# Unused bytes between the on-chip tiles of a one-core encoder layer

## The chip, the core and the metric

The kernel runs on one core of one Trainium2 chip. The time is the device time of one execution in microseconds (us). The kernel before takes 2625.61 us (median of 3 runs, 2624.94 to 2625.66).

On-chip memory has 128 partitions, and a tile lies at the same byte range of each of them. Below, "place" is the byte at which a tile starts in a partition, and "residue" is that place modulo 512. The place of a tile isn't written in the kernel: tiles of a pool follow one another in the order in which their tags first appear, pools follow one another in the order in which they are opened, and a pool that is closed gives its place to the next.

## The reference

It is one encoder layer on 256 tokens of width 2048, all in float32: a half-step feed-forward block (SwiGLU with 5632 hidden columns), a mixer, a second half-step feed-forward block, and a layer norm behind each.

```
h = LN1(alpha*h + 0.5*SwiGLU_1(h))
h = LN2(alpha*h + Mixer(h))
h = LN3(alpha*h + 0.5*SwiGLU_2(h))

def swiglu(x, w_in, w_out):
    gate, up = jnp.split(x @ w_in, 2, axis=-1)
    return (jax.nn.silu(gate) * up) @ w_out
```

The mixer projects h to 18944 columns, runs a bidirectional gated linear recurrence (16 heads) and a dilated-window attention (12 heads) on them, projects both results back with `w_branch_a` and `w_branch_b`, gates and adds them, and ends with an output projection. Nearly all the arithmetic is activations (256 tokens) times float32 weights, which are read once.

## The kernel before

**Three products for one.** Each float32 operand a is split into H, which is a rounded to the type float32r, and L = a - H, also float32r. A product of x and W is computed as xH·WH + xH·WL + xL·WH, three matmuls that add up in one PSUM bank. TensorE loads a stationary operand of 128x128 (LDWEIGHTS) and streams a moving operand past it (MATMUL), one pair of instructions for each matmul.

**The stream of weights.** `run` goes through a list of `Job`s, one for each block of 512 or 1024 output columns. A job's weights come in chunks of 128 x 2048 elements (1 MB). `load` (L148 to L170) starts the DMA of a chunk into one of 3 `raw` tiles on SP's queue, and splits it in two halves: `nc.scalar.copy` writes `wH`, `nc.vector.tensor_sub` writes `wL` (both L165, four buffers each). `load` is called a step ahead of the matmuls that use it.

**Four forms of matmul.** In most jobs (`mm`, L217) the stationary operand is 128x128 of the transposed activations and the moving one is 128x512 of the weights:

- the projections of x: `xH` and `xL` are stationary;
- the second half of each feed-forward block: `hH` and `hL`, two buffers each, which hold the transposed hidden activations of a block;
- the projections behind the mixer: `oBH` and `oBL` (attention), `xH` and `xL` once more (recurrence), and `zH` and `zL` (output projection).

The projections to the attention's columns take every second token (`parity`), so that the stationary operand has a stride of two elements. The projections that feed the recurrence (`dims`, L229) are the other way round: 128x128 of the weights is stationary, and 128x256 of `xH` or `xL` moves. The last chunks of the second feed-forward half and of the output projection put their split weights outside the pool `wsp`, into tiles named `early` that lie in the same pool as `hH` and `hL`, or as `zL`.

**What else runs.** Between the matmuls of a job, `pump` places pieces of other work: transposes (`transpose4`, L104), the recurrence (L582 to L694) and the attention. ScalarE and VectorE split activations (`split`, L109 and L110), empty PSUM and do the layer norms. Three layer norms lie between the phases.

**Where tiles lie.** The pools `const`, `wraw`, `wsp`, `big` and `small` are opened once, in that order, and `ffn1`, `oA`, `hgrn`, `m2`, `att`, `m3` and `ffn2` lie behind them in turn. The first tile of the program, `ident` (512 bytes), lies at byte 16512, and the tiles of `const` add up to 3264 bytes, so that `raw` starts at 19776. All tiles of `wraw`, `wsp` and `big` are multiples of 4096 bytes. `small` takes 1248 bytes. So:

| tile | place before | residue | place after | residue |
|---|---|---|---|---|
| raw (first) | 19776 | 320 | 19456 | 0 |
| wH, wL | 44352 on | 320 | 44032 on | 0 |
| acc | 77120 | 320 | 76800 | 0 |
| xH | 93504 | 320 | 93184 | 0 |
| xL | 109888 | 320 | 109632 | 64 |
| first pool behind `small` | 127520 | 32 | 127488 | 0 |
| hH, two buffers (first feed-forward block) | 143904, 152096 | 32, 32 | 144512, 152768 | 128, 192 |
| hL, two buffers | 160288, 168480 | 32, 32 | 161024, 169280 | 256, 320 |
| oBH, oBL, zH, zL | | 32 | | 0 |
| early beside h | | 32 | | 0 or 384 |
| early beside z | | 32 | | 0 |

The column "after" follows from the sizes of the tiles in the change below.

Of the kernel before, what the change touches and what calls it, by code (L numbers as in the profile page):

```python
# [10 lines left out]
F32 = mybir.dt.float32  # L11
F32R = mybir.dt.float32r
# [5 lines left out]
P = 128  # L18
SEQ = 256
NT = SEQ // P  # L20
D = 2048
KD = D // P
# [20 lines left out]
class Job:  # L43
    """One block of output columns: out[tok, C] = sum over nk tiles of x^T W.

    head/tail: this many of the first/last chunks run one token tile after the other.
    room: gives room for a chunk's split weights outside the pool for them, or None.
    mid: called after the first step; hook: before the last token tile meets the last chunk.
    dims: the block comes out transposed, out[col, tok], two heads to a bank.
    """  # L50

# [18 lines left out]
def kernel(ctx, tc, x, ffn1_in, ffn1_out, ln1_g, ln1_b, mix_in, lb_fwd, lb_bwd,  # L70
# [3 lines left out]
    x, out = x[0], out[0]  # L74
# [3 lines left out]
    const = ctx.enter_context(tc.tile_pool(name="const", bufs=1))  # L78
    wraw = ctx.enter_context(tc.tile_pool(name="wraw", bufs=3))
    wsp = ctx.enter_context(tc.tile_pool(name="wsp", bufs=4))  # L80
    big = ctx.enter_context(tc.tile_pool(name="big", bufs=1))
    small = ctx.enter_context(tc.tile_pool(name="small", bufs=2))
# [9 lines left out]
    acc = big.tile([P, NT, D], F32, name="acc")  # L92

    def new_x():
        return (big.tile([P, KD, SEQ], F32R, tag="xH", name="xH"),
                big.tile([P, KD, SEQ], F32R, tag="xL", name="xL"))

# [9 lines left out]
    def split(ps, H, L):  # L107
        """H + L = ps exactly, both in float32r."""
        nc.scalar.copy(out=H, in_=ps)  # L109
        nc.vector.tensor_sub(out=L, in0=ps, in1=H.bitcast(F32))  # L110

    def rsqrt(y, v, n):
        """y = v ** -0.5 for [P, n] (v is positive): a guess from the exponent and three Newton steps."""
        z = small.tile([P, n], F32, tag=f"rs{n}", name="rsz")
        nc.vector.tensor_scalar(y.bitcast(I32), v.bitcast(I32), 1, None, op0=OP.logical_shift_right)
        nc.vector.tensor_scalar(y.bitcast(I32), y.bitcast(I32), -1.0, MAGIC, op0=OP.mult, op1=OP.add)
        for i in range(3):
            if n == 1:
                nc.vector.scalar_tensor_tensor(z, y, v, y, op0=OP.mult, op1=OP.mult)
            else:  # L120
                nc.vector.tensor_mul(z, y, y)
                nc.vector.tensor_mul(z, z, v)
            # the factor -2 of each of the first two steps stays in y, and is taken out in the last
            if i < 2:
                nc.vector.scalar_tensor_tensor(y, z, -3.0 * 4.0 ** i, y, op0=OP.add, op1=OP.mult)
            else:
                nc.vector.tensor_scalar(z, z, -768.0, -1.0 / 8192.0, op0=OP.add, op1=OP.mult)
                return nc.vector.tensor_mul(y, y, z)
# [17 lines left out]

# [1 line left out]
    def load(job, r, parts=1):  # L148
# [25 lines left out]
    def fence(ins):  # L174
        """What is traced from here to the end of this step or, if that is sooner, of the next
        goes to the vector engine behind ins."""
        es = ExitStack()
        es.enter_context(tc.issue_after(ins.ins))
        fences.append([es, 2])
# [95 lines left out]
    def to_x(src, xo, t, c):  # L275
        """Columns c * 512... of token tile t, in src [P, 512], to the transposed H and L."""
        ps = transpose4([src[:, i * P:(i + 1) * P] for i in range(4)])
        ts = slice(t * P, (t + 1) * P)
        split(ps.rearrange("p (k s) -> p k s", k=4), xo[0][:, 4 * c:4 * c + 4, ts], xo[1][:, 4 * c:4 * c + 4, ts])

# [1 line left out]
    stats = {}  # L282
# [6 lines left out]
    class LayerNorm:  # L289
# [32 lines left out]
        def tile(self, t):  # L322
            """Token tile t of acc is complete."""
            if t == 1:
                for c, u in self.got.items():
                    self.apply(0, c, u)
            self.begin(t)
            if t == 0:
                if not self.lead:
                    self.apply(0, 0)  # L330
            elif self.dst is not None:
                self.rest([(1, c) for c in range(4)])
            elif self.lead:
                self.rest([(1, 0), (1, 1), (0, 2), (1, 2), (0, 3), (1, 3)])
            else:
                self.rest([(1, 0)] + [(tt, c) for c in range(1, 4) for tt in range(NT)])

        def first(self):
            """The last tile is nearly complete."""
            for c in range(2 if self.dst is None else 4):  # L340
                self.got[c] = self.scale(0, c)
# [10 lines left out]

# [1 line left out]
    def ffn(w_in, w_out, cur, pool, before, tpost, post, hook):  # L354
        blocks = [(0, 512)] + [(c, 1024) for c in range(512, DFF, 1024)]
        jobs, outs = [], []
        for bi, (c0, C) in enumerate(blocks):
            st = {}

# [11 lines left out]
            def hid(st=st, C=C):  # L371
                st["H"] = pool().tile([P, 8, SEQ], F32R, tag="hH", name="hH", bufs=2)
                st["L"] = pool().tile([P, 8, SEQ], F32R, tag="hL", name="hL", bufs=2)

                def gen():
                    for c in range(C // 512):
                        for t in range(NT):
                            to_x(st["s"][:, t, c * 512:(c + 1) * 512], (st["H"], st["L"]), t, c)
                            yield 1.2
                fast.append(gen())  # L380
# [9 lines left out]
            last = bi == len(blocks) - 1  # L390
# [15 lines left out]
        last = jobs[-1]  # L406
        last.tail, last.room, last.tpost, last.post, last.hook = 4, room, tpost, post, hook
        return jobs

    cur = {}  # L410
    stacks = []
# [9 lines left out]

# [1 line left out]
    cur["x"] = new_x()  # L423
    pl = {}
    pl["ffn"] = open_pool("ffn1")
    vecs = const.tile([P, P], F32, name="vecs")

# [53 lines left out]

# [1 line left out]
    ln = {}  # L483
# [19 lines left out]

# [1 line left out]
    hs = {}  # L505
# [42 lines left out]
    def hgrn_pair(g, pr, st):  # L548
# [15 lines left out]
        def flat(ap, t, b, f):  # L564
            """[P, h * t, u] or, for one t, [P, h, u] of half f of block b."""
            if t is None:
                return ap.rearrange("p (g b f u) -> p g b f u", b=2, f=2, u=HCHUNK)[:, :, b, f, :]
            return v6(ap)[:, :, t, b, f, :]
# [7 lines left out]
        K1, Q1, KC, QC = t512("k1"), t512("q1"), t512("kc"), t512("qc")  # L576
        # direction d: inc is the decay from the chunk's entry up to and with a token, exc the decay
        # from behind a token to the chunk's end; entry and end are those of the direction's time
        KS, QR, inc, K2, Q2 = {}, {}, {}, {}, {}
        for d in range(2):  # L580
# [22 lines left out]
            yield 1.7  # L603
            # near half: the one that the direction enters first
            nr, fr = (0, 1) if d == 0 else (1, 0)
# [6 lines left out]
        for d in range(2):  # L612
            # keys of block bk meet queries of block bq of the same tile, keys of tile bk queries of tile bq
            nr, fr = (0, 1) if d == 0 else (1, 0)
# [28 lines left out]

        # scores, keys on partitions
        def tok(ap, h, t):
# [32 lines left out]
        for h in range(2):  # L678
            hl = 2 * pr + h
            hd = 4 * g + hl  # L680
            v = st["v"]
            for t in range(NT):
                o = po[:, (2 * h + t) * P:(2 * h + t + 1) * P]
                nc.tensor.matmul(out=o, lhsT=ATd[h][:, t, :], rhs=v[:, t, hl * P:(hl + 1) * P],  # L684
                                 start=True, stop=False)
                # ATo[:, h, 0]: keys of tile 0, queries of tile 1; [:, h, 1] the other way
                nc.tensor.matmul(out=o, lhsT=ATo[:, h, 1 - t, :], rhs=v[:, 1 - t, hl * P:(hl + 1) * P],  # L687
                                 start=False, stop=True)
# [70 lines left out]

    # attention: columns of group g are q, k, v of 512; tile 0 has the even tokens and tile 1 the odd ones,  # L760
    # so that the second and third group attend only within a tile
    def parity(x, k, t):
# [75 lines left out]

    # branch gates
    def gate_evac(key, blk):  # L840
# [99 lines left out]

# [1 line left out]
    def ln3_before():  # L942
# [57 lines left out]
```

## Time and profile before

| | |
|---|---|
| time, median of 3 runs | 2625.61 us |
| profiled execution, first to last instruction (its span) | 2623.6 us |
| TensorE (PE) busy | 2600.1 us, 99%, 12889 matmuls |
| weight loads (PEld) busy | 2187.8 us, 83% |
| VectorE (DVE) busy | 1533.4 us, 58% |
| ScalarE (ACT) busy | 1155.7 us, 44% |
| read from HBM | 479.17 MB, 183 GB/s over the span |
| granted TensorE clock, mean | 0.999 |

The page of the profile gives the busy time of each engine and a chain of work that ended last. The profiled execution is known by its span; the median of the runs is 2.0 us above it. A group of instructions is named by the line of the kernel, the engine, and "out<-in" by tile names, followed by its count, its busy time and the mean duration of one. A matmul is pipelined: its recorded duration is longer than the distance from its start to the start of the next. That distance, called spacing below, is read from the chain of waits, where a row "start, us, what xN" that holds N matmuls back to back has the length N times the spacing.

### The profile page before, as it was taken

To read this page: it belongs to the slowest core of one execution; us is meant where nothing else is said; L and a number is where in the kernel's file an instruction comes from. 1 tells how busy PE (TensorE), PEld (TensorE's weight loads), DVE (VectorE), ACT (ScalarE), POOL (GpSimd) and SP (SyncE) were. 2 spreads that over 40 slices of the span, in tenths; PEclk is the share of its full clock that TensorE was granted. 3 is DMA by queue.
4 is the path that set the end of the run, shared out by engine and by line. 5 is a ranking of instruction groups with operands and counts; after the bars stand their busy time and mean duration, and the time that the engine had idled before them with its cause. 6 is when DMAs were issued, how large, how long until landed. Compare 5 with 4: busy or idle time off the path is not lost.

```text
span 2623.6 us, 31518 instructions
## 1 busy us (share of the span) xinstructions
PE 2600.1 (99%) x12889; PEld 2187.8 (83%) x12889; DVE 1533.4 (58%) x1865; ACT 1155.7 (44%) x1395; POOL 4.8 (0%) x28
## 2 busy tenths in 40 slices
PE   8999999999999999999999999999999999999998
PEld 7888888888889999998888888888788888888886
DVE  5455555454585877878544544556755455555557
ACT  5444343444444455554544544444444444444442
POOL 0000000000000000000000000000000000000000
PEclk9999999999999999999999999999999999999999
DMA  7555555555655544544555445656555555555563
GB/s 243 187 184 192 192 192 179 193 190 192 211 174 177 177 162 145 174 163 161 188 177 183 154 162 193 191 191 213 172 193 191 193 178 192 191 192 181 193 220 129
DMA packets 147281, 483.32 MB, mean 184 GB/s; under 512 B 7664, under 2 KB 7872, under 8 KB 146368
## 3 DMA queue, kind: packets, MB, share of 16 engines
q1 hardware_dynamic: 145680, 473.99, 54.4%
q10 hardware_dynamic: 1456, 7.32, 0.7%
q8 instruction: 101, 1.65, 0.2%
q14 instruction: 44, 0.36, 0.0%
HBM read 479.17 MB, written 2.10 MB: 183 GB/s over the span
## 4 chain that ended last, share of the span: by engine, by line
PE 97%; DVE 2%; DMA 0%; ACT 0%; issue 0%; SPq 0%; DVEq 0%; ACTq 0%
PE ps L217 82%; PE ps L229 10%; PE tp L104 2%; PE tp L653 1%; PE tp L657 1%; DVE wL L165 0%; DVE lnu L307 0%; PE tp L687 0%; DVE lnu L311 0%; DMA acc<-in_x 0%; PE tp L808 0%; PE tp L816 0%; DVE st L287 0%; PE tp L684 0%; PE tp L672 0%; ACT wH L165 0%
## 5 line engine op out<-in xcount | busy, mean ns | idle before, releaser
L165 DVE TENSOR_TENSOR wL<-raw,wH 128x1024 fp32r<-128x1024 f32 x884 | 1078.1, 1222 | 1007.8 <-ACT wH L165 1006.3
L165 ACT CAST wH<-raw 128x1024 fp32r<-128x1024 f32 x884 | 929.0, 1052 | 1291.5 <-PE ps L217 1157.0
L217 PE MATMUL ps<-wH,xH 128*128 128x512 f32 x2336 | 748.1, 391 | 1.7 <-ACT xH L109 1.7
L217 PE MATMUL ps<-wL,xH 128*128 128x512 f32 x2336 | 749.0, 391 | 0.0
L217 PE MATMUL ps<-wH,xL 128*128 128x512 f32 x2336 | 748.6, 391 | 0.3
L217 PEld LDWEIGHTS ps<-wH,xH 128*128 128x128 f32 x2336 | 440.0, 189 | 92.5 <-ACT xH L109 2.8
L217 PEld LDWEIGHTS ps<-wH,xL 128*128 128x128 f32 x2336 | 440.2, 189 | 92.1 <-DVE xL L110 1.8
L217 PEld LDWEIGHTS ps<-wL,xH 128*128 128x128 f32 x2336 | 439.6, 189 | 89.9
L217 PE MATMUL ps<-wL,hH 128*128 128x512 f32 x672 | 216.7, 399 | 0.0
L217 PE MATMUL ps<-wH,hH 128*128 128x512 f32 x672 | 212.0, 396 | 0.0
L217 PE MATMUL ps<-wH,hL 128*128 128x512 f32 x672 | 210.9, 395 | 0.0
L217 PEld LDWEIGHTS ps<-wH,hL 128*128 128x128 f32 x672 | 126.0, 188 | 29.8
L217 PEld LDWEIGHTS ps<-wH,hH 128*128 128x128 f32 x672 | 125.2, 188 | 29.7
L217 PEld LDWEIGHTS ps<-wL,hH 128*128 128x128 f32 x672 | 125.3, 188 | 29.0
L229 PE MATMUL ps<-xH,wH 128*128 128x256 f32 x768 | 125.8, 285 | 0.0
L229 PE MATMUL ps<-xL,wH 128*128 128x256 f32 x768 | 124.8, 284 | 0.0
L229 PE MATMUL ps<-xH,wL 128*128 128x256 f32 x768 | 124.8, 284 | 0.0
L229 PEld LDWEIGHTS ps<-xH,wH 128*128 128x128 f32 x768 | 106.5, 192 | 0.3
L229 PEld LDWEIGHTS ps<-xH,wL 128*128 128x128 f32 x768 | 106.3, 192 | 0.0
L229 PEld LDWEIGHTS ps<-xL,wH 128*128 128x128 f32 x768 | 106.3, 192 | 0.0
L385 DVE SCALAR_TENSOR_TENSOR acc<-ps,acc 128x512 f32<-128x512 f32 x96 | 60.3, 680 | 1.3 <-PE ps L217 1.3
L217 PE MATMUL ps<-wL,zH 128*128 128x512 f32 x112 | 35.4, 397 | 0.0
(181 smaller groups left out, 1244.7 us busy)
## 6 DMA issues: line engine op xcount, KB each, us to landing
raw<-in_ffn_w_in SPq DMA_DIRECT2D x175, 1024.0 KB, 5.0
raw<-in_mix_w_in SPq DMA_DIRECT2D x148, 1024.0 KB, 5.1
raw<-in_ffn_w_out SPq DMA_DIRECT2D x88, 1024.0 KB, 5.3
raw<-in_w_branch_a SPq DMA_DIRECT2D x16, 1024.0 KB, 5.3
raw<-in_mix_w_out SPq DMA_DIRECT2D x16, 1024.0 KB, 5.4
raw<-in_w_branch_b SPq DMA_DIRECT2D x4, 1024.0 KB, 5.3
gbt<-in_ln_g ACTq DMA_DIRECT2D x3, 1024.0 KB, 7.2
gbt<-in_ln_b ACTq DMA_DIRECT2D x3, 1024.0 KB, 10.0
```

The lines of the kernel that those rows point to most:

```text
L104: nc.tensor.transpose(out=ps[:, i * P:(i + 1) * P], in_=s, identity=ident)
L165: both = nc.scalar.copy(out=H, in_=s), nc.vector.tensor_sub(out=L, in0=s, in1=H.bitcast(F32))
L217: nc.tensor.matmul(out=job.ps[t, j], lhsT=job.lhs(a, k, t), rhs=b[:, o + j * 512:o + (j + 1) * 512], start=first, stop=last)
L229: nc.tensor.matmul(out=job.ps[h // 2][:, (h % 2) * SEQ:(h % 2 + 1) * SEQ], lhsT=b[:, o + h * P:o + (h + 1) * P], rhs=a[:, k, :], start=fir ...
L385: nc.vector.scalar_tensor_tensor(a, ps, 0.5, a, op0=OP.mult, op1=OP.add)
L653: nc.tensor.matmul(out=pa[:, (d * NT + t) * P:(d * NT + t + 1) * P], lhsT=tok(KS[d], h, t), rhs=tok(QR[d], h, t), start=True, stop=True)
L657: nc.tensor.matmul(out=pc[:, (i * NT + t) * P:(i * NT + t + 1) * P], lhsT=tok(a, h, t), rhs=tok(b, h, t), start=True, stop=True)
```

## The change

Unused tiles named `fill` are allocated, the tile `vecs` moves from `const` to the pool of the first feed-forward block, and the buffers of `hH` and `hL` become 64 bytes longer, with the tile used through a view of its first 8192 bytes. Nothing reads or writes the unused bytes. Comments and docstrings are taken out so that line numbers stay. No instruction is added, removed or moved.

```diff
@@ -91,9 +91,17 @@
     acc = big.tile([P, NT, D], F32, name="acc")
 
+
+    const.tile([P, 48], F32, name="fill")
+    small.tile([P, 56], F32, name="fill", bufs=1)
+
+    cur = {}
+
     def new_x():
-        return (big.tile([P, KD, SEQ], F32R, tag="xH", name="xH"),
-                big.tile([P, KD, SEQ], F32R, tag="xL", name="xL"))
+        H = big.tile([P, KD, SEQ], F32R, tag="xH", name="xH")
+        if not cur:
+            big.tile([P, 16], F32, name="fill")
+        return H, big.tile([P, KD, SEQ], F32R, tag="xL", name="xL")
...
-            st = {}
+            st = {"first": bi == 0}
...
             def hid(st=st, C=C):
-                st["H"] = pool().tile([P, 8, SEQ], F32R, tag="hH", name="hH", bufs=2)
-                st["L"] = pool().tile([P, 8, SEQ], F32R, tag="hL", name="hL", bufs=2)
+                if st["first"]:
+                    pool().tile([P, 32], F32, tag="fill", name="fill")
+                for key in "HL":
+                    a = pool().tile([P, 8 * SEQ + 16], F32R, tag="h" + key, name="h" + key, bufs=2)
+                    st[key] = a[:, 0:8 * SEQ].rearrange("p (k s) -> p k s", k=8)
...
-    cur = {}
     stacks = []
...
     cur["x"] = new_x()
     pl = {}
     pl["ffn"] = open_pool("ffn1")
-    vecs = const.tile([P, P], F32, name="vecs")
+    vecs = pl["ffn"].tile([P, P], F32, name="vecs")
```

## The prediction

> **What bounds the kernel now.** I read the page first, for the bound and the chain of work that ended last.
>
> ```profile
> span 2623.6 us, 31518 instructions
> PE 2600.1 (99%) x12889; PEld 2187.8 (83%) x12889; DVE 1533.4 (58%) x1865; ACT 1155.7 (44%) x1395; POOL 4.8 (0%) x28
> PE 97%; DVE 2%; DMA 0%; ACT 0%; issue 0%; SPq 0%; DVEq 0%; ACTq 0%
> L165 ACT CAST wH<-raw 128x1024 fp32r<-128x1024 f32 x884 | 929.0, 1052 | 1291.5 <-PE ps L217 1157.0
> ```
>
> TensorE is on 97% of the chain, and ScalarE, which splits the weights, sits idle for 1157.0 us until a matmul frees a buffer. So the kernel's time is the number of matmuls times the spacing at which they start, and only a change of that spacing can move it much. No instruction is added or removed. So I asked for the chain inside single stages, where it is one unbroken row of matmuls. Columns: start us, length us, what, count. Each row below is from a window of its own.
>
> ```profile
> 309.97 80.24 PE ps L217 x354
> 1569.93 90.21 PE ps L217 x398
> 404.99 31.03 PE ps L217 x133
> 1669.95 18.20 PE ps L217 x78
> 1789.97 60.20 PE ps L217 x258
> 1344.85 10.27 PE ps L217 x44
> 899.94 15.12 PE ps L229 x126
> ```
>
> The first two are projections of x: 80.24/354 and 90.21/398 are 226.7 ns each. The next three are the second half of a feed-forward block (h), the attention's projection (oB) and the output projection (z): 31.03/133, 18.20/78 and 60.20/258 are all 233.3 ns. The instruction and its shape are the same, 128x128 stationary and 128x512 moving, in all five. The sixth is the attention's input, with a stationary operand of every second column: 10.27/44 = 233.4 ns. The last streams 256 columns: 15.12/126 = 120.0 ns.
>
> What differs between 226.7 and 233.3? The activity beside the matmuls doesn't. These are the windows of the first (x), third (h) and fifth (z) row, with the busy time and count of PE, PEld, DVE, ACT and POOL, the clock, the DMA share and GB/s:
>
> ```profile
> 310.00:390.00 80.00, 80.00 (x354) 66.25 (x353) 37.87 (x34) 33.31 (x34) 0.00 (x0) 1.00 0.59 196
> 405.00:436.00 31.00, 31.00 (x134) 24.89 (x134) 15.77 (x15) 11.70 (x12) 0.00 (x0) 1.00 0.55 186
> 1790.00:1850.00 60.00, 60.00 (x258) 48.16 (x257) 33.15 (x32) 24.54 (x24) 0.00 (x0) 1.00 0.67 232
> ```
>
> VectorE is busy 47%, 51% and 55% of them, ScalarE 42%, 38% and 41%, and the clock is full in all. The places differ: in the stages at 226.7 ns weights and x both have residue 320, and in those at 233.3 ns the weights have 320 and h, oB and z have 32. The two are then 288 (or, the other way, 224) apart, an odd multiple of 32. One group tells place from stage: the last chunks' `early` weights, which lie at residue 32 like h and z. The view of the instructions that use hH has, in ns, minimum, median and maximum:
>
> ```profile
> L217 PE MATMUL ps<-wH,hH x672: 390/396/481, 147.0 to 2604.7; 128*128 128x512 f32 x168
> L217 PE MATMUL ps<-early,hH x64: 387/389/402, 733.7 to 2610.9; 128*128 128x512 f32 x64
> L217 PE MATMUL ps<-wH,xL x2336: 387/389/628, 13.5 to 2520.0; 128*128 128x512 f32 x195
> ```
>
> (The third row is from the same view of xL.) Recorded durations are longer than the spacing, but move with it. With the same hH as stationary operand, weights that share its residue take 389 ns, as the x stages do, and weights that don't take 396. Those 7 ns are the 6.6 ns between the spacings. So the relative place of the two operands sets the spacing, as far as this trace goes.
>
> **The change part by part.** Aligned, a matmul has spacing 226.7 ns for 512 columns and 120.0 for 256. The 256 columns between cost 106.7, so 512 columns stream in 213.3 and the rest, 13.3 ns, is paid once for each matmul. With operands an odd multiple of 32 apart it is 20.0 ns. The change can move this fixed part, between 20.0 (or more) and nothing.
>
> *Operands brought to equal residues.* oB and z go from (320, 32) to (0, 0), which is the state of the x stages. Counts:
>
> ```profile
> L217 PE MATMUL ps<-wL,oBH 128*128 128x512 f32 x32 | 10.1, 395 | 0.0
> L217 PE MATMUL ps<-wL,zH 128*128 128x512 f32 x112 | 35.4, 397 | 0.0
> L229 PE MATMUL ps<-xL,wH 128*128 128x256 f32 x768 | 124.8, 284 | 0.0
> ```
>
> Each row is one of the three products, so there are 96 and 336 matmuls: 432 x 6.64 = 2.9 us. (6.64 is 233.31 - 226.67, from the h and the first x row.) This part is the surest, since its end state is in the trace.
>
> *Operands brought to residues that differ by a multiple of 64.* hH and hL go to 128 to 320, against weights at 0: 3 x 672 = 2016 matmuls. xL goes to 64, which touches 2336 matmuls less the 288 of the strided projection (9 blocks x 16 x 2), so 2048, and the 768 of the third row above. The 96 matmuls of h with `early` weights also go from equal residues to a multiple of 64. No TensorE stream of this data type in the trace has operands 64 apart. Bounds: at worst the fixed part is 20.0, as at an odd multiple of 32; at best it is gone. The nearest row is float32 matmuls of the recurrence, where the tile order puts v at residue 288 and atd at 352, 64 apart, and wqc and wkc both at 288:
>
> ```profile
> L684 PE MATMUL tp<-v,atd x64: 275/275/275, 885.4 to 1239.8; 128*128 128x128 f32 x64
> L657 PE MATMUL tp<-wqc,wkc x64: 275/275/275, 876.3 to 1232.0; 128*128 128x128 f32 x64
> ```
>
> They take the same 275 ns. It is weak evidence, since this type streams slower and may not feel a place at all, but it is the only pair, and it says that 64 apart is as good as 0. I take 13.3 ns for every multiple of 64: h gains 2016 x 6.64 = 13.4 us, and xL and `early` stay.
>
> *Left alone.* xH against the weights keeps residue difference 0. The strided projection is already at difference 0 and at 233.4 ns, so its extra comes from the stride: nothing gained. The float32 matmuls and transposes keep their rates within a pool (275 above).
>
> *What hides the rest.* `vecs` in another pool, and the places at which DMAs, ScalarE and VectorE write, can only matter where PE waits for them. A faster PE in the h and z stages needs a 1 MB chunk in 24 x 226.7 ns = 5.44 us, and the x stages already live on that at 196 GB/s (the window at 310). If that cover were gone, PE would fall back to its present 233.3 ns at most, that is, to no gain. Ends of phases, where VectorE's layer norm is on the chain, keep their length; they start earlier.
>
> Sum: 2.9 + 13.4 = 16.3 us. Against the profiled execution: 2623.6 - 16.3 = 2607.3 us. The median of the runs is 2.0 us above the span (2625.6 against 2623.6), so **2609.3 us**.
>
> **The rivals.**
>
> *A multiple of 64 other than 0 is better than 0 (faster still).* For it: 13.3 ns of fixed part remain, and the trace never shows them gone at any place. Against it: the 275 ns pair. It touches xL (2048 + 768), h (2016) and `early` (96), 4928 matmuls; all of the 13.3 would be 65.7 us and give 2543.6, half of it 32.9 us and 2576.4 us. I take the half. The Trainium skill, TensorE: Matmul & The Clock Gate, in the section "Wait — 56ns, not 53.3ns?", has matmuls of 512 columns back to back at 215.7 ns; by that figure up to 11.0 ns could go, and an estimate of the whole gain would be 54 us more. No run here shows such a spacing.
>
> *A multiple of 64 other than 0 is worse than 0 (slower).* The point from which it decides is any distance between a stationary xL and its moving weights: equal residues may be the only cheap case, as the trace shows no other cheap one. Then xL pays 20.0 instead of 13.3, 2816 x 6.64 = 18.7 us, `early` 0.6, h stays at 233.3 and gains nothing, and only oB and z bring 2.9: 2625.6 + 16.4 = 2642.0 us. What adds to it: after a switch the spacing takes several matmuls to settle, as after the recurrence's projection here, and xL and xH at different residues switch every few matmuls.
>
> ```profile
> 847.47 0.40 PE L217 MATMUL ps<-wH,xH 128*128 128x512 f32 x1
> 847.70 0.40 PE L217 MATMUL ps<-wL,xH 128*128 128x512 f32 x1
> 847.94 0.39 PE L217 MATMUL ps<-wH,xL 128*128 128x512 f32 x1
> 848.17 0.40 PE L217 MATMUL ps<-wH,xH 128*128 128x512 f32 x1
> 848.40 0.39 PE L217 MATMUL ps<-wL,xH 128*128 128x512 f32 x1
> 848.63 0.39 PE L217 MATMUL ps<-wH,xL 128*128 128x512 f32 x1
> 848.86 0.39 PE L217 MATMUL ps<-wH,xH 128*128 128x512 f32 x1
> ```
>
> The starts are 0.23, 0.24, 0.23, 0.23, 0.23 and 0.23 apart: 1.39 us for six, against 1.36 at 226.7.
>
> *Place isn't the cause (no change).* The 6.6 ns would belong to something else in those stages, and the time stays at 2625.6 us. Against it stand the 389 of `early` with hH and the like activity in the windows. The Trainium skill speaks for it: TensorE: Matmul & The Clock Gate, section "Step-by-step: what each phase is for", says that loading the next weights doesn't steal read bandwidth from the running matmul, since the two have ports of their own. By that rule the place of two tiles could cost nothing; the 396 against 389 ns disagree.
>
> **How the numbers follow.** The forecast has 0.50, the better offsets 0.22, the worse offsets 0.14, place without effect 0.10, and 0.04 are for mixtures near it. About 0.2% of 2625.6, or 5 us, is what a measurement can tell from no change. Faster by more: 0.50 + 0.22 and most of the mixtures, 0.75; within: 0.11; slower: 0.14. The forecast's own range is 2605 to 2613 (h from 11 to 15 us, since the settling after transposes doesn't shrink). The whole range goes down to 2574, which takes in the half of the fixed part, and up to 2630, which takes in no change and leaves out the worse offsets; beyond the ends lie about 0.09 and 0.11.
>
> **What would show it.** If I am right, the chain in an h stage has 226.7 ns a matmul, hH's median duration falls from 396 to 389, x stages keep 226.7, the strided projection 233.4 and the recurrence's 120.0, and ScalarE's wait for matmuls shrinks by about the gain. A spacing below 226 in the h stages or where xL is stationary shows the first rival, one above 230 where xL is stationary the second, and 233.3 in the oB and z stages the third. The forecast is wrong if any of the 64-multiples has a spacing of its own.

## The result, and the profile after

The changed kernel takes 2640.19 us (median, 2640.01 to 2640.68) against 2625.28 us of the kernel before on the same chip: a ratio of 1.0058, 95% interval 1.0043 to 1.0072. It is slower. The prediction was 2609.3 us, with a range of 2574 to 2630, so it had the wrong sign. Its second rival, which gave 2642.0 us, came nearest.

The page of the changed kernel has the same number of instructions on each engine, and only TensorE's busy time has grown by more than 2 us (line numbers are 8 to 10 higher):

```profile
span 2637.9 us, 31519 instructions
PE 2615.2 (99%) x12889; PEld 2189.6 (83%) x12889; DVE 1534.4 (58%) x1865; ACT 1153.1 (44%) x1395; POOL 4.8 (0%) x28
PE 97%; DVE 2%; DMA 0%; ACT 0%; issue 0%; SPq 0%; DVEq 0%; ACTq 0%
L173 ACT CAST wH<-raw 128x1024 fp32r<-128x1024 f32 x884 | 926.4, 1049 | 1308.6 <-PE ps L225 1175.2
```

PE is 15.1 us busier (2615.2 against 2600.1) and ScalarE, in its splits of the weights, waits for it 18.2 us longer (1175.2 against 1157.0). The chain of waits inside single stages (start us, length us, what, count; one window for each row) says where:

```profile
1584.96 90.13 PE ps L225 x390
411.85 28.37 PE ps L225 x121
544.92 30.27 PE ps L225 x131
1681.91 18.19 PE ps L225 x80
1802.88 59.16 PE ps L225 x261
1349.97 10.12 PE ps L225 x44
789.99 60.12 PE ps L237 x508
```

| stage | matmuls | ns each before | after | us |
|---|---|---|---|---|
| x (xH at 0, xL at 64 from the weights) | 6144 | 226.7 | 231.1 | +27.0 |
| h, blocks at 128 and 256 / at 192 and 320 | 2016 | 233.3 | 234.5 / 231.1 | -1.0 |
| oB and z (0) | 432 | 233.3 | 227.4 / 226.7 | -2.8 |
| strided | 864 | 233.4 | 230.0 | -2.9 |
| the recurrence's projection | 2304 | 120.0 | 118.3 | -3.8 |

The spacings come from the rows above and from those of the kernel before; h is taken at the mean of its two kinds of block, 232.8 ns. The sum is +16.5 us against +14.3 us between the spans (2637.9 - 2623.6); 1.2 us of the difference is the first DMA of the chain, which is 6.59 us long instead of 7.75. Two rows of the table were not in any forecast: the strided and the recurrence's projection became faster.

The views of the instructions that use xL and hH show it on single matmuls (minimum/median/maximum ns):

```profile
L225 PE MATMUL ps<-wH,xL x2336: 387/397/500, 12.4 to 2534.5; 128*128 128x512 f32 x195
L225 PE MATMUL ps<-wH,hH x672: 387/395/482, 147.6 to 2618.9; 128*128 128x512 f32 x168
L225 PE MATMUL ps<-early,hH x64: 388/394/399, 740.3 to 2625.2; 128*128 128x512 f32 x64
```

The medians were 389, 396 and 389: xL and `early` lost what they had, and hH gained next to nothing.

### The profile page after: what moved, and what is told of

Same layout as the page of the kernel before. It is cut to its first block, busy times and chain, and to the rows that moved or that the text cites. A ratio compares the mean times of both kernels' runs of the same rounds, so it can differ in the third digit from the quotient of the medians.

```text
span 2637.9 us, 31519 instructions
## 1 busy us (share of the span) xinstructions
PE 2615.2 (99%) x12889; PEld 2189.6 (83%) x12889; DVE 1534.4 (58%) x1865; ACT 1153.1 (44%) x1395; POOL 4.8 (0%) x28
## 4 chain that ended last, share of the span: by engine, by line
PE 97%; DVE 2%; DMA 0%; ACT 0%; issue 0%; SPq 0%; DVEq 0%; ACTq 0%
PE ps L225 83%; PE ps L237 10%; PE tp L112 2%; PE tp L663 1%; PE tp L667 1%; DVE wL L173 0%; DVE lnu L315 0%; PE tp L697 0%; DVE lnu L319 0%; PE tp L818 0%; PE tp L826 0%; DVE st L295 0%; DMA acc<-in_x 0%; PE tp L694 0%; PE tp L682 0%; ACT wH L173 0%
## 5 line engine op out<-in xcount | busy, mean ns | idle before, releaser
L173 ACT CAST wH<-raw 128x1024 fp32r<-128x1024 f32 x884 | 926.4, 1049 | 1308.6 <-PE ps L225 1175.2
L225 PE MATMUL ps<-wH,xL 128*128 128x512 f32 x2336 | 758.8, 396 | 0.3 <-DVE xL L118 0.3
L225 PE MATMUL ps<-wL,xH 128*128 128x512 f32 x2336 | 757.1, 395 | 0.0
```

What stands on the lines that cost most here:

```text
L173: both = nc.scalar.copy(out=H, in_=s), nc.vector.tensor_sub(out=L, in0=s, in1=H.bitcast(F32))
L225: nc.tensor.matmul(out=job.ps[t, j], lhsT=job.lhs(a, k, t), rhs=b[:, o + j * 512:o + (j + 1) * 512], start=first, stop=last)
```

## The experiments

The theories at the start: **S**, a stationary operand whose residue differs from that of the one before it upsets a settled rhythm; **O**, a distance other than 0 between the stationary operand and its moving weights is dear by itself; **A**, residue 0 of the weights is worse than 320. The runs were made on three chips, on which the kernel before took 2625.1 to 2625.7 us, so their times are compared with one another.

### Everything at one residue

```diff
-    small.tile([P, 56], F32, name="fill", bufs=1)
+    small.tile([P, 72], F32, name="fill", bufs=1)
...
-        if not cur:
-            big.tile([P, 16], F32, name="fill")
...
-                if st["first"]:
-                    pool().tile([P, 32], F32, tag="fill", name="fill")
...
-                    a = pool().tile([P, 8 * SEQ + 16], F32R, tag="h" + key, name="h" + key, bufs=2)
+                    a = pool().tile([P, 8 * SEQ + 0], F32R, tag="h" + key, name="h" + key, bufs=2)
```

> Every operand of the float32r matmuls at residue 0: weights, xH, xL, hH, hL, oB, z. Theory S (a stationary operand whose residue differs from that of the one before it upsets the settled rhythm) and theory O (a distance of 64 to 320 bytes between the stationary operand and its moving weights is dear by itself) expect the same here: x and h both 226.7 ns a matmul, 2609 us by my first sum, and up to 5 us less if the gains of the changed kernel in the recurrence's projection (119.3 for 120.0 ns) and the strided one (230.4 for 233.3) belong to the place of the weights. Theory A (residue 0 of the weights itself is worse than 320) expects x near 231 ns and 2635 us or more.

Measured: 2610.49 us (2609.76 to 2611.13), ratio to the kernel before 0.9943, interval 0.9928 to 0.9958. Chain rows of an x, an h, the recurrence's and a strided stage:

```profile
311.98 76.16 PE ps L223 x336
402.99 31.05 PE ps L223 x137
789.96 40.08 PE ps L235 x334
1290.91 10.27 PE ps L223 x44
```

x is at 226.7 and h at 226.6 ns. The recurrence's 120.0 and the strided 233.4 are those of the kernel before, although every place has changed from residue 320 to 0. So theory A falls, and what counts is the distance. The equal-distance part of the prediction holds to about 1 us.

### Both halves of x at 64

```diff
+        if not cur:
+            big.tile([P, 16], F32, tag="fillp", name="fill")
         H = big.tile([P, KD, SEQ], F32R, tag="xH", name="xH")
-        if not cur:
-            big.tile([P, 16], F32, name="fill")
...
-                    pool().tile([P, 32], F32, tag="fill", name="fill")
+                    pool().tile([P, 16], F32, tag="fill", name="fill")
                 for key in "HL":
+                    if st["first"] and key == "L":
+                        pool().tile([P, 96], F32, tag="fillm", name="fill")
```

> Weights at 0, xH and xL both at 64, hH and hL of a block both at 64 or both at 128: every stationary operand has a distance to its weights that isn't 0, but none differs from the one before it. Theory S: settled rhythm, x and h near 226.7 ns, about 2609 us. Theory O: x at 231 ns or above (6144 matmuls x 4.4 = 27 us) and h near 233: 2638 us or more.

Measured: 2653.23 us (2652.91 to 2654.8), ratio 1.0107, interval 1.0092 to 1.0122. Chain rows of x, h at 64, h at 128, the recurrence's and a strided stage:

```profile
314.98 82.13 PE ps L225 x352
409.83 34.30 PE ps L225 x147
544.78 35.23 PE ps L225 x151
799.97 50.06 PE ps L237 x425
1349.94 10.12 PE ps L225 x44
```

x, h at 64 and h at 128 are all at 233.3 ns with nothing to switch between. Theory S falls as the whole story and O stands: a distance of 64 bytes costs as much as the 288 (or 224) of the kernel before. For the other two forms the sign is opposite: 117.8 against 120.0 ns in the recurrence's projection, 230.0 against 233.4 in the strided one.

### x alone, h alone

The first keeps the layout of the changed kernel for x and puts h at 0, the second the reverse.

```diff
# x alone
-                    pool().tile([P, 32], F32, tag="fill", name="fill")
...
-                    a = pool().tile([P, 8 * SEQ + 16], F32R, tag="h" + key, name="h" + key, bufs=2)
+                    a = pool().tile([P, 8 * SEQ + 0], F32R, tag="h" + key, name="h" + key, bufs=2)
# h alone
-    small.tile([P, 56], F32, name="fill", bufs=1)
+    small.tile([P, 72], F32, name="fill", bufs=1)
...
-        if not cur:
-            big.tile([P, 16], F32, name="fill")
```

> xH at 0 and xL at 64 as in the changed kernel; hH and hL at 0. Both theories: x at 231.1 ns as in the changed kernel, h at 226.7 ns instead of 232.6 (2016 x 5.9 = 12 us): about 2628 us.

> xH and xL at 0; hH at 128 and 192, hL at 256 and 320 as in the changed kernel. Both theories: x at 226.7 ns, h at 232.6: about 2609 + 12 = 2621 us. With the run before it this splits the loss between x and h; the two shares, 25 us for x and 12 us for h against the state with all at 0, should add up to the 31 us between that state and the changed kernel, within the 5 us that are open for the projections.

Measured: 2629.61 us (2629.01 to 2630.73) and 2622.06 us (2620.36 to 2622.92). Against 2610.49 us with all at one residue, x costs 19.1 us and h 11.6 us, together 30.7; the changed kernel is 29.7 us above that state. The parts add up to within 1 us, so little else was lost. I had put x at 25 us; the 6 us between are about what the recurrence's and the strided projection gain with xL at 64 (6.7 us in the table).

### Distances 256, 448 and 32

Only the unused tiles change, in size and place; with x at 256, for instance:

```diff
+        if not cur:
+            big.tile([P, 64], F32, tag="fillp", name="fill")
         H = big.tile([P, KD, SEQ], F32R, tag="xH", name="xH")
...
-                    a = pool().tile([P, 8 * SEQ + 16], F32R, tag="h" + key, name="h" + key, bufs=2)
+                    a = pool().tile([P, 8 * SEQ + 48], F32R, tag="h" + key, name="h" + key, bufs=2)
```

> Theory S has fallen: with both x tiles steadily at 64 the x stages took 233.3 ns. Two forms of theory O remain. O1: for a contiguous stationary operand only equal residues are cheap, and every other distance costs about 233. O2: the cheap distances recur at a shorter period than 512. Here weights at 0, xH and xL at 256, hH and hL both at 192 or both at 384. O1: x and h near 233 ns: 2610.5 + 40 (x) + 13 (h) - 9 (recurrence's and strided projections, which were faster at a distance of 64) = 2654 us. O2 with period 256 or 128: x at 226.7 ns, and about 2615 us.

> Weights at 0, x at 448 (64 the other way round), h at 96 or 320, oB and z at 192. O1: everything contiguous near 233 ns, about 2610.5 + 40 + 13 + 3 - 9 = 2657 us. If the sign of the distance matters (a stationary operand 64 ahead of its weights is dear, 64 behind them cheap), x stays at 226.7 ns and the time is about 2618 us.

> Weights at 0, x at 32, h at 256 or 448. O1: x and h near 233 ns, 2654 us, so that an odd multiple of 32 is no worse than a multiple of 64 (my prediction held 64 for harmless and 32 for dear). O2 with period 256: the blocks with h at 256 at 226.7 ns, 6 us less.

Measured: 2618.26 us, 2627.97 us and 2643.72 us (the last from two executions). Chain rows with x at 256 (x, h at 192, h at 384):

```profile
309.89 78.20 PE ps L225 x345
404.80 29.30 PE ps L225 x128
539.89 27.18 PE ps L225 x117
```

With x at 448 (x, h at 320, the recurrence's, oB at 192):

```profile
309.98 80.11 PE ps L225 x350
409.98 27.07 PE ps L225 x116
799.98 45.11 PE ps L237 x398
1666.80 17.40 PE ps L225 x76
```

With x at 32 (x, h at 256, h at 448):

```profile
312.79 83.30 PE ps L225 x357
409.83 32.19 PE ps L225 x142
544.85 32.27 PE ps L225 x141
```

In ns a matmul: 256 gives 226.7 for x and 226.7 for h. 448 gives 228.9 for x and for h, and 192 gives 228.9 for h and oB. 320 gives 233.4, as 64 does, and 384 gives 232.3 where 128 gave 233.3. So distances repeat, nearly, with a period of 256, and neither O1 (only equal residues modulo 512) nor the idea that only the sign matters holds. My prices for x at 448 were wrong for that reason: 228.9 is between cheap and dear. So was that for x at 32, 2654 us less 6: the blocks with h at 448 take 228.9 ns and not the 233 that I had given them, which on some 1000 matmuls is the 4 us between 2648 and 2643.72.

### Half the changes between xH and xL

Layout of the run with x alone; the order of the three products is turned round in some groups.

```diff
                     for t in range(NT):
-                        for k, a, b, o, first, last in g:
+                        back = (k + t) % 2 == 1 and 0 < k < job.nk - 1
+                        for k, a, b, o, first, last in g[::-1] if back else g:
```

> xH at 0, xL at 64, h at 0 as in the run with the x tiles alone (2629.6 us), but every second group of six matmuls runs its three products in reverse order, so that xL meets xL and xH meets xH: half as many changes between the two residues (plain projections only). If the 15 us that matmuls of xH lose there (4027 x (230.6 - 226.9)), though their own distance is 0, come from the neighbourhood of xL, some 5 us come back: about 2624 us, with xH near 229 ns and xL a little slower than 232.1. If each matmul's time depends on its own distance alone, nothing changes: 2629.6 us.

Measured: 2629.62 us (2628.62 to 2630.44), no different from 2629.61. The edit did less than I had said: two turned groups also follow each other, so that of 8 changes in four groups 6 remain. By its time alone the run speaks for the second case, that each matmul goes by its own distance. But in the projections of x, xH averages 226.8 ns from start to start where all is at one residue, and 230.6 beside xL at 64, at the same distance of its own. So the neighbour counts. In this run xH has 230.3, where I had expected 229: fewer changes were not shown to bring time back. TensorE's timeline shows the rhythm (start us, us, what, count), from one xL to the next:

```profile
1606.29 0.63 PE L225 MATMUL ps<-wH,xL 128*128 128x512 f32 x2
1606.75 0.62 PE L225 MATMUL ps<-wL,xH 128*128 128x512 f32 x2
1607.21 1.09 PE L225 MATMUL ps<-wH,xH 128*128 128x512 f32 x4
1608.14 0.61 PE L225 MATMUL ps<-wL,xH 128*128 128x512 f32 x2
1608.59 0.63 PE L225 MATMUL ps<-wH,xL 128*128 128x512 f32 x2
```

From start to start, the eight matmuls of xH take 0.46 us for the first two, 0.93 for the next four and 0.45 for the last two: 230, 232.5 and 225 ns each. This rhythm, six dear and two cheap, returns in 161 of the 249 such stretches of the trace; in the other 88 each of the eight averages 228 to 232 ns. So behind matmuls at a distance of 64, several at distance 0 pass before they are cheap, if they get there. In the changed kernel xH has two or four in a row, and averages 230.6 ns.

### 256 in the place of 64

```diff
-    small.tile([P, 56], F32, name="fill", bufs=1)
+    small.tile([P, 8], F32, name="fill", bufs=1)
...
-            big.tile([P, 16], F32, name="fill")
+            big.tile([P, 64], F32, name="fill")
```

hL is put 256 bytes behind hH in the same way.

> xH and hH at residue 0, xL and hL at 256: the same change as the one under study, with 256 in the place of 64. Theory O2 with period 256: x and h 226.7 ns, 2610.5 us. If it is the alternation of two residues as such that upsets the rhythm, xH falls to 230.6 ns as it did beside xL at 64, and the time is 2625 us or more.

Measured: 2610.79 us (2610.21 to 2611.16), ratio 0.9943, interval 0.9928 to 0.9958. Chain rows of x and h:

```profile
309.86 77.29 PE ps L225 x341
403.82 29.24 PE ps L225 x129
```

Both are at 226.7 ns. Alternating between two residues costs nothing when both distances are multiples of 256. That settles what was wrong with the change: not unequal residues as such, but distances that aren't multiples of 256.

### A map of distances

In the next two runs the two halves of a split chunk lie in one tile that is 512 bytes longer than both, at an offset that each job of the mixer's projections may choose; `hmask` moves to the recurrence's pool to make room.

```diff
-                H = wsp.tile([P, HALF], F32R, tag="wH", name="wH")
-                L = wsp.tile([P, HALF], F32R, tag="wL", name="wL")
+                w = wsp.tile([P, 2 * HALF + 128], F32R, tag="w", name="w")
+                H, L = (w[:, job.off + i * HALF:job.off + (i + 1) * HALF] for i in range(2))
```

> All activations at one residue, and in the mixer's projections the split weights lie at a chosen offset in a longer tile, another one for each job: 10 plain jobs, 12 of the recurrence's projection (there the weights are stationary) and 5 strided ones. It maps spacing against distance (stationary minus moving, modulo 256). From the runs so far: plain 226.7 at 0, 233.3 at 64, 232.5 at 128, 229.0 at 192, 233 to 234 at 32, 96 and 224; recurrence 120.7 at 0, 115.8 at 64, 118.0 at 192 and 224; strided 233.3 at 0, 230.1 at 64. Theory O2 (each distance modulo 256 has a spacing of its own) expects a smooth course through these points, 228 to 235 ns for the plain jobs, and the recurrence's best near 64. No plain distance should be below 226.7 by it; one that is would leave room below my forecast. The time is a mixture and tests nothing.

Its time, 2615.66 us in one run, is a mixture. Chain rows of plain jobs at distances 16, 248, 144 and 176, then of the recurrence's at 64 and 48, then strided ones at 64 and 96:

```profile
1532.28 43.63 PE ps L224 x187
1577.08 43.63 PE ps L224 x187
1049.19 21.04 PE ps L224 x91
944.68 21.03 PE ps L224 x91
881.82 9.54 PE ps L236 x84
817.61 22.45 PE ps L236 x182
1265.19 38.19 PE ps L224 x166
1353.48 42.48 PE ps L224 x182
```

Plain: 233.3, 233.3, 231.2 and 231.1 ns. So even 8 bytes on one side (248 is 8 short of 256) and 16 on the other lose all of the gain, and no distance I tried lies below 226.7. The course isn't smooth as I had expected: 192 with 228.9 is the next lowest, then 144 and 176 with 231. The recurrence's projection has 113.6 ns at 64 and 123.4 at 48 in these stretches; strided jobs have 230.1 at 64 and 233.4 at 96.

### Each form at its own best distance

```diff
+    OFF = {'plain': {}, 'dims': {'all': 64}, 'strided': {'all': 192}}
```

> As the run with everything at one residue (2610.5 us), but each form of matmul gets the distance that was best for it: 0 for the plain ones, 64 for the recurrence's projection (weights 64 bytes further on), 64 for the strided one (weights 192 further on). Theory O2: 2304 x (120.7 - 115.8) = 11.3 us and 864 x (233.3 - 230.1) = 2.8 us less: 2596 us. If those gains came with the place of x itself and not with the distance, 2610 us.

Measured: 2599.42 us (2599.1 to 2601.14), ratio 0.9902, interval 0.9886 to 0.9919: the fastest version, 40.8 us below the changed kernel. Chain rows of x, h, two stages of the recurrence's projection and two strided ones:

```profile
309.98 78.20 PE ps L224 x345
402.80 30.37 PE ps L224 x134
779.96 55.12 PE ps L236 x468
1125.11 16.90 PE ps L236 x149
1349.81 10.35 PE ps L224 x45
1318.85 20.30 PE ps L224 x87
```

x and h stay at 226.7 and 226.6 ns. The recurrence's projection is at 117.8 ns in the first of its stretches and at 113.4 in the second, and the strided one at 230.0 and at 233.3, although each form has one distance throughout. So for these two forms the distance alone doesn't set the spacing; what else does is open. The gain of 11.1 us over the state at one residue is 3 us short of the 14.1 expected. Over all its blocks the recurrence's projection averages 115.5 ns from start to start, against 119.9 with all at one residue, which is some 10 us where I had 11.3; one of the five strided blocks, the one at 1318.85, didn't gain; the last microsecond or so isn't accounted for.

## Why the prediction was wrong

- *What bounds the kernel, and that place sets the spacing.* Right. No instruction changed, and the runs moved the time between 2610 and 2653 us by places alone. The rival "place isn't the cause" is out. At the same shapes, 226.7 or 233.3 ns follow the distance between the two operands, so the load and the stream are not independent of each other here. The Trainium skill (TensorE: Matmul & The Clock Gate, "Step-by-step: what each phase is for") says that loading the next weights doesn't steal read bandwidth from the running matmul; the runs disagree with it as far as independence goes, and whether bandwidth is what is lost no run shows.
- *Operands brought to equal residues.* Right: oB and z fell from 233.3 to 227 ns. With all operands so, the kernel takes 2610.5 us, 1.2 us from the 2609.3 that I had forecast for the changed one.
- *"I take 13.3 ns for every multiple of 64."* This is the step that failed. I read the odd multiple of 32 between the slow pairs as the cause, and took 64 for harmless from one pair of float32 rows at 275 ns, which I had called weak. The rows of before had only two distances, 0 and 288 or 224, and can't tell a period of 64 from one of 256. The cheap distances are the multiples of 256; 64 has 233.3 ns (the run with both halves of x at 64). So h kept its fixed part of about 20 ns (232.8 on average, a gain of 1.0 us for 13.4 predicted) and xL lost the cheap state that it had: its matmuls average 232.1 ns, and x as a whole, put at nothing, cost 27.0 us.
- *"xL and `early` stay."* Wrong with it (the median of `early` with hH rose from 389 to 394 ns), and xL took xH along. That rival 2 came out at 2642.0 us is in part luck: it priced xL's own loss, and left the settling beside it without a price. The settling is why x as a whole is at 231.1 ns, though two thirds of its matmuls are xH at distance 0. Against it stood gains that it hadn't either, 2.9 us in the strided and 3.8 us in the recurrence's projection.
- *"The strided projection ... nothing gained" and the recurrence's rate unchanged.* Wrong. Both feel the distance, and of those tried 64 is better for them than 0. The recurrence's 113.4 ns lie below the 106.7 + 13.3 that the prediction had split 120.0 into, so 13.3 ns isn't a fixed part that the two forms share.
- *What hides the rest.* Right: ScalarE's wait for matmuls grew and shrank with PE's time (1175.2 us in the changed kernel, 1140.4 with all at one residue), and PE kept 97% of the chain in both.
- *The better offsets.* Half right for a reason I didn't give: nothing below 226.7 was seen for the plain form, but the recurrence's projection does better at 64 than at 0.

## What to carry to other kernels

Where TensorE's chain is unbroken, divide its length by its count stage by stage: a few ns between stages of the same shape point to where the operands lie. For this type and shape, keep the stationary and the moving operand a multiple of 256 bytes apart, all of them, since one operand at a bad distance slows its neighbours too; xL at 64 and h at 128 to 320 are what cost 30 us here. A distance that the trace doesn't contain has no price yet: one run with each form of matmul at several distances, set by an offset into a longer tile, buys a first map. Take more than one stage for each distance, as the recurrence's stages at one distance differ by 4 ns.

## What the runs showed of the hardware that was not expected

- The spacing of a float32r matmul with 512 moving columns, a contiguous stationary operand and its own weight load depends on (stationary place - moving place) modulo 256: 226.7 ns at 0, 228.9 at 192, 231 to 235 at the other distances tried, the closest being 8 bytes from a multiple of 256.
- It has a memory: behind two or four matmuls at a distance of 64, the first six at 0 average 230.8 ns and the next two 227.2 (249 stretches of the run with fewer changes). A change between 0 and 256 has no such effect (2610.79 us).
- With 256 moving columns the order of distances is another: 120.0 ns at 0, about 113 to 118 at 64, 123.4 at 48. With a stationary stride of two elements 0 is among the dearest (233.4) and 64 the best of those tried (230.0, but 233.3 in one block).
- Why the period is 256, and what the two operands share on their way to the array, is open; no run here looks inside it. In every stage that the argument rests on, both halves of the weights lie at one residue, so it is open too whether a load meets its own matmul's moving operand or that of the matmul running at the time.
